# Neighbourhood attention in query blocks of 8 rows by 16 columns: key blocks of 12 by 32, values reloaded by block, one bias table per block

## The chip, the core and the metric

The kernel runs on one core of one Trainium2 chip. The metric is the time of one launch on the device, in microseconds (us). A core has engines that run their own instruction streams in order and wait for each other by semaphores: TensorE (PE, matrix products; its weight loads are listed as PEld), VectorE (DVE), ScalarE (ACT), GpSimd (POOL) and SyncE (SP, which here issues the DMA transfers). Engines compute on SBUF, 128 partitions wide; PE writes to PSUM banks of 512 fp32 columns.

## The reference

Two blocks run one after the other on 1024 tokens of width 1024. The first, in which the change lies, normalises the input, projects it, and joins two branches by an output projection: neighbourhood attention (8 heads of 64) and a gated delta rule (4 heads of 128, two directions). The tokens form a grid of 16 rows by 64 columns. Each query attends to a window of 8 rows by 16 columns around it, clipped at the borders, with a learned bias per offset:

```python
cs = np.clip(cols - NA_KW // 2, 0, GRID_W - NA_KW)      # 16 columns
rs = jnp.clip(r - kh // 2, 0, rows - kh)                # 8 rows
s = jnp.einsum('bhwd,bhiwjd->bhwij', q_r, k_sel).astype(jnp.float32) * scale + bias.astype(jnp.float32)
p = jax.nn.softmax(s.reshape(B, H, GRID_W, kh * NA_KW), axis=-1).reshape(s.shape).astype(v.dtype)
return jnp.einsum('bhwij,bhiwjd->bhwd', p, v_sel)
...
attn = _neighbourhood_attention(aq, ak, heads(av, NA_HEADS), rpb) * jax.nn.silu(az)
```

q and k are RMS-normalised per head with a gain. The delta rule needs, per chunk of 128, direction and head, inverses of triangular 64x64 blocks, their merging to 128x128, and a scan over the chunks. The second block (stick-breaking attention, retention, merge) is not touched.

## The kernel before

The program is written as loops of generators that are advanced in turn; a scheduler then fixes the order of each engine's instructions from its own model of their times, so the order around the change is not written out by hand.

The attention is made in four head pairs p. `na_proj(p)` (L479 to L524) projects q, k, v in token tiles of 128 (`dense_tok`, L102: fp32 values as a rounded part and a rest, three passes, 24 matmuls a tile) and the gate z in columns (L112, 48 matmuls of 512 columns). It squares (L496), sums (L498), takes the root on POOL, copies q, k, v out of PSUM on ACT (L501 to L503), scales q and k on DVE (L506), transposes k for four tiles at once (L514) and keeps it as rounded part and rest kS (L517, L518). It loads a bias table of 128x22x64 per head (L489).

`na_attn(p)` (L526 to L616) goes through eight query tiles of two grid rows, 128 queries. Its keys are eight whole grid rows, 512 columns; masked ones carry a large negative bias. Per tile q is doubled (L534), transposed (L537) and split (L539, L540). Per head two matmuls of 512 columns make the scores (L552); DVE adds the bias and takes the maximum (L560), negates it (L562), ACT takes the exponential and its sum (L563). Of four of the eight tiles the two rows have different windows: a second score matmul (L556) and short value matmuls (L589, evacuated at L598, added at L599) serve the eighth row. One tile later the probabilities are transposed (L569, four per head) and copied (L571), and multiplied with v (L583; each shows as two records, one per 64 columns of weights, in part). The sums' reciprocal (L591) is spread (L593), transposed (L594) and multiplied into the gate z (L595), which then multiplies the values (L600 or L602).

Other work runs between. `solver()` (L452 to L475) inverts by updates of X, each a product (L463) and an addition (L465), on DVE with buffer svt and on POOL with svq; the last rows on DVE with svq. The driver (L627 to L638) advances it four steps per tile of pairs 0 and 1, with the projection of the next pair; behind pair 1 comes `dz_raw` (L618), 192 matmuls of 256 columns. During pair 2 `merges()` (L655 to L693) makes eight merges, each a chain L668 (PE), L670 (ACT), L673 (PE), L676 (DVE), L679 (PE), L681 (ACT), for the last four also L687 (PE), in three PSUM banks "a" that the projections use too. During pair 3 the scan (L695 to L807) runs in 16 steps that each load 1.5 MB.

## Time and profile before

| | us |
|---|---|
| median of 3 runs (2333.69 to 2344.59) | 2336.43 |
| span of the profiled execution; no time of its own is recorded beside it | 2331.9 |
| PE busy | 2182.4 (94%) |
| DVE busy | 1414.8 (61%) |
| ACT busy | 863.7 (37%) |
| POOL busy | 1252.0 (54%) |
| DMA | 240.86 MB, mean 103 GB/s |

Busy times are sums over the whole span, and stages differ. The changed stage is about the fifth of the span between 300 and 760 us. A group's mean length is that of its instructions one by one; matmuls overlap, so the distance between two starts is shorter than a length.

### The profile page before, as it was taken

Reading aid. Unit: us, or ns where it says so; the run is one execution under the profiler, and the core shown is the slowest. Engines: PE = TensorE matmul, PEld = TensorE weight load, DVE = VectorE, ACT = ScalarE, POOL = GpSimd, SP = SyncE. Lnnn points to the kernel's source line nnn. Section 1 sums busy time; section 2 is a strip of 40 time slices with the busy share of each in tenths; the row PEclk is TensorE's granted clock in tenths of the full one; section 3 lists DMA queues with packets and bytes.
Section 4 is the critical chain, followed back from the end, with each engine's and each line's share of the span. In section 5 each row is a group of like instructions: output and inputs, shape, how many; then the busy total and the mean of one; then the engine's idle time right before and its main releaser. Section 6 shows DMA issues by size and latency. Waiting matters only on the chain.

```text
span 2331.9 us, 33715 instructions
## 1 busy us (share of the span) xinstructions
PE 2182.4 (94%) x12069; PEld 1864.4 (80%) x12069; DVE 1414.8 (61%) x2596; ACT 863.7 (37%) x2126; POOL 1252.0 (54%) x1467
## 2 busy tenths in 40 slices
PE   7998888999999999899889999999999999989999
PEld 7776877787888798787788777788888888767887
DVE  4688789844456568887877784426474744343221
...
GB/s 131 80 170 166 203 80 26 37 165 132 154 279 205 153 84 46 50 55 55 10 50 50 55 50 72 72 56 46 64 46 64 46 82 91 226 213 211 140 109 108
DMA packets 236488, 240.86 MB, mean 103 GB/s; under 512 B 39776, under 2 KB 173600, under 8 KB 236064
## 3 DMA queue, kind: packets, MB, share of 16 engines
...
q14 instruction: 73, 0.60, 0.1%
HBM read 167.31 MB, written 71.34 MB: 102 GB/s over the span
## 4 chain that ended last, share of the span: by engine, by line
PE 33%; DVE 16%; POOL 7%; issue 4%; DMA 4%; ACT 4%; SPq 0%; POOLq 0%; ACTq 0%; DVEq 0%
PE acc L112 21%; PE acc L102 5%; DVE qf L132 4%; PE acc L859 3%; DVE A L1039 3%; POOL A L1044 2%; DMA raw<-in_w_in_dram 1%; POOL wu L71 1%; DVE A L1035 1%; POOL ss L126 1%; DMA oa<-d_oa 1%; DVE ob L132 1%; DVE sq L988 1%; DVE wT L1058 1%; PE pt L1160 1%
## 5 line engine op out<-in xcount | busy, mean ns | idle before, releaser
L112 PE MATMUL acc<-h2h,wu 128*128 128x512 f32 x1504 | 459.1, 396 | 6.7 <-DVE sq L988 2.7
L102 PE MATMUL acc<-wu,h2h 128*128 128x384 f32 (+1 forms) x1536 | 376.2, 327 | 13.4 <-DVE sq L988 4.2
L71 POOL TENSOR_TENSOR wu<-raw,wu 128x512 fp32r<-128x512 f32 (+3 forms) x268 | 363.4, 1365 | 6.3
L70 POOL TENSOR_SCALAR wu<-raw 128x512 fp32r<-128x512 f32 (+3 forms) x268 | 205.9, 772 | 250.7 <-PE acc L112 176.7
L112 PEld LDWEIGHTS acc<-h2h,wu 128*128 128x128 f32 x1504 | 281.5, 188 | 71.9 <-ACT lg L956 3.1
L102 PEld LDWEIGHTS acc<-wu,h2h 128*128 128x128 f32 x1536 | 272.2, 194 | 21.5 <-issue 3.5
L112 PE MATMUL acc<-h2l,wu 128*128 128x512 f32 x752 | 276.1, 396 | 0.0
L102 PE MATMUL acc<-wu,h2l 128*128 128x384 f32 (+1 forms) x768 | 250.1, 327 | 0.0
L102 PE MATMUL acc<-wu,h1hi 128*128 128x384 f32 (+2 forms) x768 | 193.1, 335 | 12.6 <-DVE kS L518 6.7
L112 PE MATMUL acc<-h1hi,wu 128*128 128x512 f32 x512 | 164.3, 409 | 8.0 <-ACT pad L315 4.7
L112 PEld LDWEIGHTS acc<-h2l,wu 128*128 128x128 f32 x752 | 141.4, 188 | 31.0
L102 PEld LDWEIGHTS acc<-wu,h1hi 128*128 128x128 f32 x768 | 138.5, 196 | 17.0 <-issue 8.0
L1044 POOL TENSOR_TENSOR A<-Z,A 128x128 f32<-128x128 f32 (+2 forms) x96 | 112.4, 1176 | 70.5 <-DVE A L1039 43.6
L102 PEld LDWEIGHTS acc<-wu,h2l 128*128 128x128 f32 x768 | 148.4, 193 | 1.0
L102 PE MATMUL acc<-wu,h1lo 128*128 128x384 f32 (+2 forms) x384 | 127.8, 335 | 0.0
L112 PEld LDWEIGHTS acc<-h1hi,wu 128*128 128x128 f32 x512 | 98.1, 193 | 33.0 <-ACT pad L315 6.2
L126 POOL TENSOR_TENSOR ss<-ss,mhalf 128x2 f32<-128x2 f32 (+2 forms) x136 | 115.6, 851 | 7.2
L132 DVE STREAM_TRANSPOSE qf<-sq 32x256 f32<-32x256 f32 x256 | 111.6, 436 | 4.0
L125 POOL TENSOR_SCALAR ss<-ss 128x2 f32<-128x2 f32 (+2 forms) x136 | 42.5, 312 | 117.7 <-ACT sq L982 47.0
L1060 PE MATMUL po<-wT,v 128*128 128x512 f32 (+3 forms) x288 | 76.1, 365 | 22.2 <-DVE wT L1058 12.2
L112 PE MATMUL acc<-h1lo,wu 128*128 128x512 f32 x256 | 96.4, 405 | 0.0
L112 PE MATMUL acc<-oah,wu 128*128 128x512 f32 x256 | 81.3, 413 | 10.0 <-DVE sg L1232 6.1
...
## 6 DMA issues: line engine op xcount, KB each, us to landing
raw<-in_w_in_dram SPq DMA_DIRECT2D x192, 256.0 KB, 2.8
...
```

The source lines that it names most:

```text
L70: nc.gpsimd.tensor_scalar(out=u[:, 0, :], in0=raw, scalar1=1.0, scalar2=0.0, op0=ALU.mult, op1=ALU.add)
L71: nc.gpsimd.tensor_tensor(out=u[:, 1, :], in0=raw, in1=f32(u[:, 0, :]), op=ALU.subtract)
L102: nc.tensor.matmul(acc[:, :n], lhsT=hT[a][:, k, m * P:(m + 1) * P], rhs=us[k][:, b, c0:c0 + n], start=(k == 0 and i == 0), stop=(k == NK - ...
L112: nc.tensor.matmul(accs[half], lhsT=us[k][:, b, c0:c0 + P], rhs=hT[a][:, k, half * 512:(half + 1) * 512], start=(k == 0 and i == 0), stop= ...
L125: nc.gpsimd.tensor_scalar(out=dst, in0=src, scalar1=mul, scalar2=eps, op0=ALU.mult, op1=ALU.add)
L126: nc.gpsimd.tensor_tensor(out=dst, in0=dst, in1=mhalf[:, :eshape], op=ALU.pow)
L132: nc.vector.transpose(out=dst[32 * b:32 * b + 32, :, :, 32 * a:32 * a + 32], in_=src[32 * a:32 * a + 32, :, :, 32 * b:32 * b + 32])
L859: nc.tensor.matmul(acc, lhsT=us[k][:, y, (b % 4) * P:(b % 4 + 1) * P], rhs=token_set(mT[x][:, k, 0:T], s), start=(k == 0 and i == 0), stop ...
L988: nc.vector.scalar_tensor_tensor(out=sq[:, a * P:(a + 1) * P], in0=acc[:, a * P:(a + 1) * P], scalar=ss[:, a:a + 1], in1=gqk[:, a, :], op0 ...
L1039: nc.vector.tensor_tensor_scan(out=A[:, :w][:, ::-1], data0=A[:, :w][:, ::-1], data1=A[:, :w][:, ::-1], initial=0.0 if diag else ini[:, i4 ...
L1044: nc.gpsimd.tensor_tensor(out=A[:, :w], in0=Z[:, :w], in1=A[:, :w], op=ALU.subtract)
L1060: nc.tensor.matmul(po[:, i0 * P:512], lhsT=v[a][:, c0 // P + kb, :], rhs=wT[b][:, :n], start=(diag and kb == 0 and x == 0), stop=(diag == ...
```

## The change

A query tile becomes a block of 8 rows by 16 columns. All its windows lie in one key block of 12 rows by 32 columns, 384 columns, so there is one window per tile and no second matmuls. The bias comes as a table per tile for both heads, 128x2x384, with the mask in it, loaded tile by tile. Since a tile's keys are no run of tokens, v goes to DRAM (d_vn, 64 KB per token tile) and comes back by tile in the order of the key block (vb, four transfers of 32 partitions). q is normalised with its gain, doubled and transposed in the projection, four tiles at once, and kept as rounded part qH per head and rest qL. The probabilities are divided by their sum before they are transposed (one reciprocal and one scaling per head), so z is multiplied once. Line numbers move: L560 to L569, L563 to L572, L569 to L580, L583 to L591, L591 to L576, L668 to L664. The scratch memory for DMA descriptors and two tags of tiles that other stages reuse change names or size.

```diff
-    gq = load_const("qk_gain_q", [P, 1])
+    gqr = load_const("qk_gain_q", [P, 64], src=I["qk_gain_q"].partition_broadcast(P))
-    nc.vector.tensor_scalar_mul(out=gq, in0=gq, scalar1=0.125)
+    nc.vector.tensor_scalar_mul(out=gqr, in0=gqr, scalar1=0.125)
...
+    KR = (0, 4)
+    KC = (0, 8, 24, 32)
+    d_vn = dram.tile([4, T, P], F32, name="d_vn")
+    def blocks(ap):
+        return ap.rearrange("p (c r w) -> p r c w", c=4, r=8)
+    def rows(ap):
+        return ap.rearrange("p (r c w) -> p r c w", r=8, c=4)
     def na_proj(p, hold):
         us = load_units(I["w_in"], 128 * p, 128, parts=4, stride=512)
         pl = (na1, na)[p % 2]
-        qn = pl.tile([P, NM, P], F32, tag="qn", name="qn")
+        qH = [pl.tile([P, T], F32R, tag="qh%d" % hh, name="qH") for hh in range(2)]
+        qL = pl.tile([P, T], F32R, tag="ql", name="qL")
         kS = [pl.tile([P, T], F32R, tag="kS%d" % hh, name="kS") for hh in range(2)]
-        v = pl.tile([P, NM, P], F32, tag="v", name="v")
         z = pl.tile([P, T], F32, tag="z", name="z")
-        TB = []
-        for hh in range(2):
-            tb = na.tile([P, 22, 64], F32, tag="tb", name="tb", bufs=2)
-            nc.sync.dma_start(out=tb, in_=I["rpb"][2 * p + hh])
-            TB.append(tb)
-        hold.append((qn, kS, v, z, TB))
-        kns = []
+        hold.append((qH, kS, qL, z))
+        kns, qds = [], []
         for m, acc in dense_tok(hT, us, 0, 384):
             j = m % 4
             sq = na1.tile([P, 256], F32, tag="sq", name="sq", bufs=2)
             nc.scalar.activation(out=sq, in_=acc[:, 0:256], func=AF.Square)
+            raw = na1.tile([P, 384], F32, tag="raw", name="raw", bufs=2)
+            nc.scalar.copy(out=raw, in_=acc[:, 0:384])
+            nc.sync.dma_start(out=d_vn[p, m * P:(m + 1) * P, :], in_=raw[:, 256:384])
             ss = na1.tile([P, 4], F32, tag="ss", name="ss", bufs=2)
             nc.vector.tensor_reduce(out=ss, in_=sq.rearrange("p (h d) -> p h d", h=4), op=ALU.add, axis=AX.X)
             rsqrt_small(ss, ss, 1.0 / 64, EPS, 4)
             kn = na1.tile([P, P], F32, tag="kn", name="kn", bufs=5)
-            nc.scalar.copy(out=qn[:, m, :], in_=acc[:, 0:128])
-            nc.scalar.copy(out=kn, in_=acc[:, 128:256])
-            nc.scalar.copy(out=v[:, m, :], in_=acc[:, 256:384])
-            for x, t_ in enumerate((qn[:, m, :], kn)):
-                t_ = t_.rearrange("p (h d) -> p h d", h=2)
-                nc.vector.tensor_tensor(out=t_, in0=t_, in1=ss[:, 2 * x:2 * x + 2].unsqueeze(2).to_broadcast([P, 2, 64]),
-                                        op=ALU.mult)
+            nc.vector.tensor_tensor(out=kn.rearrange("p (h d) -> p h d", h=2), in0=raw[:, 128:256].rearrange("p (h d) -> p h d", h=2),
+                                    in1=ss[:, 2:4].unsqueeze(2).to_broadcast([P, 2, 64]), op=ALU.mult)
+            qd = na1.tile([P, 2, 2, 64], F32, tag="qd", name="qd", bufs=5)
+            for hh in range(2):
+                nc.vector.scalar_tensor_tensor(out=qd[:, hh], in0=raw[:, hh * 64:hh * 64 + 64].unsqueeze(1).to_broadcast([P, 2, 64]),
+                                               scalar=ss[:, hh:hh + 1], in1=gqr.unsqueeze(1).to_broadcast([P, 2, 64]),
+                                               op0=ALU.mult, op1=ALU.mult)
             kns.append(kn)
+            qds.append(qd)
             if j == 3:
                 sl = slice((m - 3) * P, (m + 1) * P)
-                # head 0 keeps its rounded part above the rest, head 1 the other way round
                 pt = bank("a")
                 for jj, k_ in enumerate(kns):
                     nc.tensor.transpose(pt[:, jj * P:(jj + 1) * P], k_, ident)
@@ -517,102 +528,87 @@
                     nc.scalar.activation(out=kS[hh][a, sl], in_=pt[a, :], func=AF.Copy, scale=gk[a])
                     nc.vector.scalar_tensor_tensor(out=kS[hh][b, sl], in0=pt[a, :], scalar=gk[a],
                                                    in1=f32(kS[hh][a, sl]), op0=ALU.mult, op1=ALU.subtract)
-                kns = []
+                for hh in range(2):
+                    a = slice(hh * 64, hh * 64 + 64)
+                    pt = bank("a")
+                    for jj, q_ in enumerate(qds):
+                        nc.tensor.transpose(pt[:, jj * P:(jj + 1) * P], q_[:, hh].rearrange("p x d -> p (x d)"), ident)
+                    nc.scalar.copy(out=blocks(qH[hh][:, sl]), in_=rows(pt))
+                    nc.vector.tensor_tensor(out=blocks(qL[a, sl]), in0=rows(pt[a, :]), in1=blocks(f32(qH[hh][a, sl])),
+                                            op=ALU.subtract)
+                kns, qds = [], []
             yield 1
         for half, acc in enumerate(dense_col(hT, us, 384)):
             last_na[0] = nc.scalar.activation(out=z[:, half * 512:half * 512 + 512], in_=acc, func=AF.Silu)
         yield 1
     def na_attn(p, tiles):
...
+        qH, kS, qL, z = tiles[p]
+        grid = lambda ap: ap.rearrange("p (r c) -> p r c", c=64)
+        def loads(t):
+            r, c = t // 4, t % 4
+            tb = na.tile([P, 2, 384], F32, tag="tb", name="tb", bufs=3)
+            nc.sync.dma_start(out=tb, in_=I["rpb"][p, t])
+            vb = na.tile([P, 3, P], F32, tag="vb", name="vb", bufs=3)
+            src = d_vn[p].rearrange("(g r c) d -> r c g d", r=4, c=64)
+            for i in range(4):
+                nc.sync.dma_start(out=vb[i * 32:i * 32 + 32], in_=src[i, KC[c]:KC[c] + 32, r:r + 3, :])
+            return tb, vb
+        def scores(t, hh, ld, rs2):
+            r, c = t // 4, t % 4
+            a = slice(hh * 64, hh * 64 + 64)
+            qs = lambda ap: ap[:, t * P:(t + 1) * P]
+            ks = lambda ap: grid(ap)[:, KR[r]:KR[r] + 12, KC[c]:KC[c] + 32]
             ps = bank("z")
...
+            nc.tensor.matmul(ps[:, 0:384], lhsT=qs(qH[hh]), rhs=ks(kS[hh]), start=True, stop=False)
+            nc.tensor.matmul(ps[:, 0:384], lhsT=qs(qL[a]), rhs=ks(kS[hh][a]), start=False, stop=True)
+            s = na.tile([P, 384], F32, tag="s", name="s", bufs=4)
             mx = na.tile([P, 1], F32, tag="mx", name="mx", bufs=4)
...
+            nc.vector.tensor_tensor_reduce(out=s, in0=ps[:, 0:384], in1=ld[0][:, hh, :],
                                            scale=1.0, scalar=-3.0e38, op0=ALU.add, op1=ALU.max, accum_out=mx)
             nc.vector.tensor_scalar_mul(out=mx, in0=mx, scalar1=-1.0)
             nc.scalar.activation(out=s, in_=s, func=AF.Exp, bias=mx, accum_out=rs2[:, hh:hh + 1])
...
+            return s
+        def transposed(s, rs2, hh):
+            nc.vector.reciprocal(out=rs2[:, hh:hh + 1], in_=rs2[:, hh:hh + 1])
+            nc.vector.tensor_scalar_mul(out=s, in0=s, scalar1=rs2[:, hh:hh + 1])
             pt = bank("t")
...
+            for i in range(3):
                 nc.tensor.transpose(pt[:, i * P:(i + 1) * P], s[:, i * P:(i + 1) * P], ident)
...
+            PT = na.tile([P, 384], F32, tag="PT", name="PT", bufs=3)
+            nc.scalar.copy(out=PT, in_=pt[:, 0:384])
             return PT
...
+        def values(t, ld, PTs):
+            r, c = t // 4, t % 4
+            po = bank("op"[t % 2])
+            for g in range(3):
                 for hh in range(2):
                     hs = slice(hh * 64, hh * 64 + 64)
...
+                    nc.tensor.matmul(po[hs, 0:P], lhsT=ld[1][:, g, hs], rhs=PTs[hh][:, g * P:(g + 1) * P],
+                                     start=(g == 0), stop=(g == 2))
+            zt = grid(z)[:, 8 * r:8 * r + 8, 16 * c:16 * c + 16]
+            nc.vector.tensor_tensor(out=zt, in0=po[:, 0:P].rearrange("p (r c) -> p r c", c=16), in1=zt, op=ALU.mult)
+        lds = [loads(0), loads(1)]
         prev = None
         for t in range(NM):
...
+            rs2 = na.tile([P, 2], F32, tag="rs2", name="rs2", bufs=3)
+            s0 = scores(t, 0, lds[t], rs2)
             if prev:
...
+                PTs = [transposed(prev[2], prev[4], 0)]
+            s1 = scores(t, 1, lds[t], rs2)
             if prev:
...
+                PTs.append(transposed(prev[3], prev[4], 1))
+                values(prev[0], prev[1], PTs)
+            if t + 2 < NM:
+                lds.append(loads(t + 2))
+            prev = (t, lds[t], s0, s1, rs2)
             yield 1
...
+        values(prev[0], prev[1], [transposed(prev[2], prev[4], 0), transposed(prev[3], prev[4], 1)])
         nc.sync.dma_start(out=d_att[p], in_=z)
```

The scheduler orders the program anew. On DVE, in pair 0, before, between solver updates (L463, L465): one tile's reciprocal, its spreading (rb), and the split of the next tile's q.

```order
L465 TENSOR_TENSOR X<-X,svt 128x10x35
L591 RECIPROCAL rs_3496<-rs_3496 128x2
L506 TENSOR_TENSOR qn<-qn,ss 128x128
L506 TENSOR_TENSOR kn<-kn,ss 128x128
L463 TENSOR_TENSOR svt<-X 128x360
L593 COPY rb<-rs_3496 128x128
L540 SCALAR_TENSOR_TENSOR qS<-pp,c_qk_gain_q,qS 128x256
L465 TENSOR_TENSOR X<-X,svt 128x10x36
L463 TENSOR_TENSOR svt<-X 128x324
L465 TENSOR_TENSOR X<-X,svt 128x9x36
```

After, a head's scores (s, mx), their negated maximum, reciprocal and scaling:

```order
L569 ISA s,mx<-pz,tb 128x384
L569 ISA mx 128x1
L463 TENSOR_TENSOR svt<-X 128x484
L571 TENSOR_SCALAR mx<-mx 128x1
L465 TENSOR_TENSOR X<-X,svt 128x44x11
L576 RECIPROCAL rs_2861<-rs_2861 128x1
L463 TENSOR_TENSOR svt<-X 128x264
L577 TENSOR_SCALAR s<-s,rs_2861 128x384
L465 TENSOR_TENSOR X<-X,svt 128x22x12
```

The reciprocal and the scaling of s now stand one or two solver updates behind the negation.

On PE, before, in pair 1: score (pz), value (pp) and transposing matmuls of a tile stand between matmuls of dz (wu, 256 columns).

```order
L552 MATMUL pz<-kS,qS 128x512 x2
L102 MATMUL acc<-wu,h1lo_99 128x256
L102 MATMUL acc<-wu,h1hi_98 128x256 x2
L552 MATMUL pz<-kS,qS 128x512 x2
L583 MATMUL pp<-PT,v 64x128 x2
L556 MATMUL pz<-kS,q_4319 64x64 x2
L583 MATMUL pp<-PT,v 64x128 x5
L589 MATMUL po<-PT,v 64x64 x4
L594 MATMUL pp<-ident,rb 128x128
L102 MATMUL acc<-wu,h1lo_99 128x256
L102 MATMUL acc<-wu,h1hi_98 128x256 x2
```

After, the end of pair 1: its gate columns (L112), the last transposes and the first value matmul, and the beginning of dz (256 columns):

```order
L112 MATMUL acc<-h1lo_99,wu 128x512 x2
L112 MATMUL acc<-h1hi_98,wu 128x512 x4
L112 MATMUL acc<-h1lo_99,wu 128x512 x2
L112 MATMUL acc<-h1hi_98,wu 128x512 x2
L580 MATMUL pt<-ident,s 128x128 x3
L591 MATMUL pp<-PT,vb 64x128
L102 MATMUL acc<-wu,h1hi_96 128x256 x2
```

The last five value matmuls of pair 1 stand 27 matmuls further on; behind them come 165 matmuls of dz without attention between, 32 of the projection of pair 3 with the scores of two tiles of pair 2 between them, and the first merge.

On PE, before, the first merge (its tiles tt, x1t, wt) and the work of the attention between its links:

```order
L668 MATMUL acc<-ident,tt 64x64 x8
L537 MATMUL po<-ident,qd 128x128 x2
L569 MATMUL pt<-ident,s 128x128 x4
L583 MATMUL pp<-PT,v 64x128
L673 MATMUL acc<-x1t,n_5227 64x64 x8
L552 MATMUL pz<-kS,qS 128x512 x4
L583 MATMUL pp<-PT,v 64x128 x7
L594 MATMUL pp<-ident,rb 128x128
L679 MATMUL acc<-tt,wt 64x64 x8
L668 MATMUL acc<-ident,tt 64x64 x8
```

After, the sixth merge, with nothing between its links:

```order
L664 MATMUL acc<-ident,tt 64x64 x8
L669 MATMUL acc<-x1t,n_5836 64x64 x8
L675 MATMUL acc<-tt,wt 64x64 x8
L683 MATMUL acc<-ident,tt 128x128 x8
L102 MATMUL acc<-wu,h1hi_96 128x384 x2
```

In the first four merges of the new order attention or projection stands between the links in part, in the last four hardly any.

## Rows read from the trace of the kernel before

**Rows 1.** Head of the page: span.
```profile
span 2331.9 us, 33715 instructions
```

**Rows 2.** Stretches: us; busy PE, PEld, DVE, ACT, POOL (xinstructions); PEclk, DMA share, GB/s.
```profile
300.00:460.00 160.00, 140.99 (x840) 119.22 (x839) 151.44 (x339) 65.14 (x179) 130.05 (x184) 0.95 0.14 44
460.00:520.00 60.00, 60.00 (x473) 52.60 (x471) 23.93 (x84) 25.92 (x62) 37.44 (x56) 1.00 0.47 140
520.00:620.00 100.00, 94.61 (x833) 78.70 (x833) 47.07 (x144) 55.48 (x135) 17.69 (x24) 0.98 0.42 127
620.00:760.00 140.00, 138.84 (x1067) 122.70 (x1066) 80.04 (x218) 68.79 (x183) 30.62 (x56) 1.00 0.70 243
```

**Rows 3.** Groups by line, 297 to 465: busy us, mean ns | idle before, releasers.
```profile
L465 DVE TENSOR_TENSOR X<-X,svt 128x294 f32<-128x294 f32 (+32 forms) x83 | 54.8, 661 | 1.4
L463 DVE TENSOR_TENSOR svt<-X 128x294 f32<-128x294 f32 (+32 forms) x83 | 53.0, 638 | 1.6
```

**Rows 4.** Timeline of PE, 655 to 675: start us, run us, line, tile, count.
```profile
656.15 0.60 PE L569 MATMUL pt<-ident,s 128*128 128x128 f32 x4
656.59 1.06 PE L719 MATMUL acc<-S,wsa 128*128 128x128 f32 x8
...
665.58 1.12 PE L583 MATMUL po<-PT,v 128*64 128x128 f32 x12
666.39 0.33 PE L589 MATMUL pp<-PT,v 64*64 64x64 f32 x4
...
666.76 0.33 PE L594 MATMUL po<-ident,rb 128*128 128x128 f32 x1
666.92 0.83 PE L740 MATMUL acc<-wsc,wsb 128*128 128x128 f32 x6
...
673.53 1.18 PE L552 MATMUL pz<-kS,qS 128*128 128x512 f32 x4
674.54 0.27 PE L569 MATMUL pt<-ident,s 128*128 128x128 f32 x1
```

**Rows 5.** Timeline of PE around the first merges, 519 to 529.
```profile
519.36 0.51 PE L102 MATMUL acc<-wu,h1hi 128*128 128x384 f32 x2
519.71 0.34 PE L102 MATMUL acc<-wu,h1lo 128*128 128x384 f32 x1
519.98 0.64 PE L668 MATMUL acc<-ident,tt 64*64 64x64 f32 x8
...
527.01 0.63 PE L668 MATMUL acc<-ident,tt 64*64 64x64 f32 x8 [0.67 <-ACT tt L681]
...
528.90 0.27 PE L673 MATMUL acc<-x1t,n 64*64 64x64 f32 x1 [0.46 <-ACT x1t L670]
```

**Rows 6.** Groups by line and shape, 290 to 740.
```profile
L563 ACT ACTIVATE s<-s,mx 128x512 f32<-128x512 f32 x64 | 46.0, 720 | 40.6 <-DVE mx L562 40.5
L552 PE MATMUL pz<-kS,qS 128*128 128x512 f32 x128 | 45.2, 444 | 0.8 <-ACT qS L539 0.6 <-DVE qS L540 0.2
L560 DVE CUSTOM_DVE_ANT_0 s<-pz,tb 128x512 f32<-128x512 f32 x64 | 42.2, 686 | 28.4 <-PE pz L552 15.3 <-PE pz L556 13.0
...
L593 DVE COPY rb<-rs 128x128 f32<-128x128 f32 x32 | 11.1, 348 | 0.4
...
L506 DVE TENSOR_TENSOR qn<-qn,ss 128x128 f32<-128x128 f32 x25 | 10.7, 426 | 5.6 <-POOL ss L126 5.3
L518 DVE SCALAR_TENSOR_TENSOR kS<-acc,c_qk_gain_k,kS 64x512 fp32r<-64x512 f32 x14 | 10.5, 750 | 1.6 <-ACT kS L517 1.3
...
L540 DVE SCALAR_TENSOR_TENSOR qS<-po,c_qk_gain_q,qS 128x256 fp32r<-128x256 f32 x16 | 7.7, 480 | 8.4 <-ACT qS L539 8.3
...
L591 DVE RECIPROCAL rs<-rs 128x2 f32<-128x2 f32 x32 | 5.1, 160 | 16.6 <-ACT s L563 16.4
```

**Rows 7.** The same over the whole span, a scaling in layer 2.
```profile
L1030 DVE TENSOR_SCALAR A<-Z 128x384 f32<-128x384 f32 x16 | 6.7, 420 | 6.3 <-PE pp L1055 3.5 <-ACT Z L1028 2.6
```

**Rows 8.** Line L593: durations ns min/median/max, first and last start.
```profile
L593 DVE COPY rb<-rs x32: 209/227/1665, 321.1 to 714.3; 128x128 f32<-128x128 f32 x32
```

More of the change, by code (lines that the diff above doesn't have):

```diff
@@ L574, in values @@
-        def values(t, st, PTs, pe):
-            po, qS, q2, rs2, rl, ru = st
-            v0 = rl // 2
-            steps = [(slice(0, P), slice(i * P, (i + 1) * P), v0 + i) for i in range(4)]
-            if rl != ru:
-                steps = steps[1:] + [(slice(64, P), slice(0, P), v0)]
-            for x, (ks, cs, vb) in enumerate(steps):
+            PT = na.tile([P, 384], F32, tag="PT", name="PT", bufs=3)
+            nc.scalar.copy(out=PT, in_=pt[:, 0:384])
+            return PT
+        def values(t, ld, PTs):
+            r, c = t // 4, t % 4
+            po = bank("op"[t % 2])
+            for g in range(3):
@@ L581, in values @@
                 for hh in range(2):
                     hs = slice(hh * 64, hh * 64 + 64)
-                    nc.tensor.matmul(po[hs, 0:P], lhsT=v[ks, vb, hs], rhs=PTs[hh][ks, cs], start=(x == 0), stop=(x == 3))
-            zt = z[:, t * P:(t + 1) * P]
-            if rl != ru:
-                for r in range(2):
-                    for hh in range(2):
-                        hs = slice(hh * 64, hh * 64 + 64)
-                        nc.tensor.matmul(pe[hs, P + r * 64:P + r * 64 + 64], lhsT=v[0:64, v0 + 4 * r, hs],
-                                         rhs=PTs[hh][0:64, r * 64:r * 64 + 64], start=True, stop=True)
@@ L610, in na_attn @@
             if prev:
-                PTs.append(transposed(prev[3]))
-                values(prev[0], prev[1], PTs, st[0])
-            prev = (t, st, s0, s1)
+                PTs.append(transposed(prev[3], prev[4], 1))
[3 more added lines that the diff above has]
+            prev = (t, lds[t], s0, s1, rs2)
             yield 1
-        values(prev[0], prev[1], [transposed(prev[2]), transposed(prev[3])], None)
+        values(prev[0], prev[1], [transposed(prev[2], prev[4], 0), transposed(prev[3], prev[4], 1)])
@@ L638, in tile_kernel @@
         dz_raw((range(0), range(0, NM))[p])
-    for g, tag in ((0, "z"), (1, "v")):
+    for g, tag in ((0, "z"), (1, "kS0")):
         zt = na.tile([P, 4, 2, P], F32, tag=tag, name="zt")
@@ L697, in scan @@
         tags = scan_tags
-        oparts = [na1.tile([P, 2, 4, P], F32, name="oacc", tag=tag) for tag in ("kS0", "kS1", "qn", "z")]
+        oparts = [na1.tile([P, 2, 4, P], F32, name="oacc", tag=tag) for tag in ("kS0", "kS1", "qh0", "z")]
         oacc = lambda n: oparts[n // 2][:, n % 2]
```

77 lines of the change are left out of this document (14 added, 63 removed).

## The prediction

> **What bounds the kernel now.** I read the page first: TensorE (PE) is busy almost throughout, so a change that removes matmuls looks like a gain. The reader should not stop there, because the share is a mean over stages. The changed stage lies between about 300 and 760 us of a span of 2331.9 us [rows 1]. I cut it where its other work changes [rows 2]. In stretch A, up to 520 us, attention of head pairs 0 and 1 runs beside the solver for the 64x64 inverses. In its first 160 us VectorE (DVE) is busy 151.44 us, 95%, against 140.99 of PE; from 460 to 520 PE is busy without a gap and DVE for 23.93 of 60 us. In B, 520 to 620, pair 2 runs beside the merges, and PE is busy 94.61 of 100. In C, 620 to 760, pair 3 runs beside the scan with PE busy 138.84 of 140, and there the DMA share is 0.70. So a matmul saved counts in C, counts in B if something else fills the merges' waits, and counts in A only where DVE is not the limit. Why DVE is full in A is in the groups of the solver: 54.8 + 53.0 us in two lines [rows 3].
>
> The sum is made against the span of the profiled execution; the median of the runs, 2336.43, lies 4.5 us above that, and I add these 4.5 at the end.
>
> **PE, removed and added.** I price by the distance between starts where matmuls stand packed, since their own lengths overlap. Four score matmuls of 512 columns take 674.54 - 673.53 = 1.01 us [rows 4], four transposes 0.44, and twelve value matmuls 0.81, 0.068 each; from the first value matmul of a tile with two row windows to its L594 it is 1.18, and L594 takes 0.16. A tile before is therefore 1.01 for scores, 0.07 for the second window's scores (four short ones on half of the tiles, priced at half a value matmul), 8 x 0.11 = 0.88 for transposes, 1.13 for values (16 x 0.068 = 1.08 or 1.18) and 0.16: 3.25 us. After, the scores have 384 columns; two L102 of 384 columns take 519.71 - 519.36 = 0.35 [rows 5], so four are 0.70; six transposes 0.66; twelve value matmuls 0.81. That is 2.17 us, 1.08 saved, 35 us over 32 tiles. The upper end is by the mean busy time: 444 ns for a score matmul [rows 6] would make it 1.78 instead of 1.01, but half of that is overlap; the ratio of 0.353 busy per matmul (45.2 / 128) to 0.253 is 1.4, which gives 1.5 per tile, 48 us. Groups of different matmuls rarely stand packed, so I take 1.3: 42 us in all, 10.4 per head pair. The q transposes move from the attention to the projection with equal count and cost nothing more.
>
> **DVE, removed and added, per tile** [rows 6]. Removed: a quarter of two L560, 2 x 0.686 x 0.25 = 0.34; qn (L506) 0.43; qS (L540) 0.48; rb (L593) 0.35; one multiply of z and, on half of the tiles, the addition L599, each priced as rb: 0.35 + 0.17. Sum 2.12. Added: two products for the normalised, doubled q (new L515), each at the price of qn, 0.86; qL, two instructions of 64x512 in four tiles at L518's 0.75, 0.38; one more reciprocal 0.16 (L591); and two multiplications of the probabilities, 128x384, which L1030 does in 0.42 [rows 7]: 0.84. Sum 2.24. DVE is given 0.12 us more per tile: what PE is spared, DVE is not. For L577 I hold 0.2 to 1.7 as bounds, the shortest and longest rb [rows 8]; 0.42 is the nearest row, of its exact shape.
>
> [...]
>
> **Stretch A.** DVE is busy 151.44 + 23.93 = 175.4 us there. The order shows that the solver's tail on svq, 20 small instructions, now stands behind pair 1's last tile; at half the mean of the solver's lines [rows 3], 0.33 each, these are 6.5 us. Up to pair 1's last scaling DVE has 169 us, plus 16 x 0.12 = 2. Its idle time of 160 - 151.44 = 8.6 I halve, since L560 waits for PE above all (28.4 us in the whole stage [rows 6]) and PE is lighter. So the last scaling comes at 300 + 171 + 4 = 475. Behind it PE still has, by the order: 48 matmuls of z with 512 columns (0.23 each from the 0.175 of 384 columns, 11.2 us), 192 of dz with 256 columns (0.117 each, 22.4), which before stood between the tiles, 32 of 384 columns (5.6), and scores and transposes of two tiles (3). These 42 us run alone, less 2 beside the last tile: the first merge comes at 515, against 519.98 [rows 5]. Of 16 tiles x 1.3 = 21 us, 5 arrive. The granted clock is 0.95 in the first part of A, where PE has gaps, and 1.00 where it has none [rows 2]; more gaps may lower it, which is hidden as long as DVE leads.
>
> **Stretch B.** Saved 10.4. Each merge is a chain of PE, ACT, PE, DVE, PE, ACT; before, attention and projection stand between the links. The distance from the end of L668 (527.01 + 0.63) to L673 at 528.90 is 1.26 us [rows 5], a link with its evacuation. The new order has merges 4 to 7 with most links back to back: about 11 unfilled links, 13.9 us. Of these 5.4 are not new, PE being idle 100 - 94.61 before [rows 2]. The twelve k and q transposes in one batch go through the three banks that the merges use also: two more links, 2.5. Sum 10.4 + 5.4 - 13.9 - 2.5, about -0.6.
>
> **Stretch C.** Saved 10.4. The eight tables (393 KB) and eight value blocks (197 KB) less two old tables (721 KB) are 3.3 MB more, where 0.70 of the DMA moves 243 GB/s [rows 2]: at full share 9.4 us. Nothing lost and 9.4 lost are the bounds; since 0.30 is free I take 3. The loads stand in order on SP two tiles ahead with three buffers; if one waits for its buffer, the scan's loads queue behind it. +7.4.
>
> ACT loses copies and a quarter of the exponentials and evacuations; at 65.14 of 160 us in A it is no bound, and I count nothing. GpSimd (POOL) has nothing new.
>
> **Sum.** 5 - 0.6 + 7.4 = 12: span 2320, and 2324 with the 4.5 us outside.
>
> **Rivals.**
> 1. The PE saving arrives whole. For it: PE's share in B, C and from 460. It needs DVE in A to get room, by L577 and L515 costing half. 42 us less: 2294. Against it: dz behind the tiles.
> 2. Slower: DVE waits for the exponential. Before, one reciprocal a tile (L591) stands well behind its exponentials, and still waited 16.4 us for ACT. Now reciprocal and scaling of each head can stand one or two solver instructions, 0.65 us each [rows 3], behind L571, while the exponential alone takes 0.720 us [rows 6] and its accumulator is read after it. The solver's next instructions are queued behind such a wait on DVE, POOL's half of the solver behind those, and PE's transposes behind the scaling. With 32 in A, the 12 us of gain are gone from 0.4 us each on; at 0.8 us each, 26 us, the time is 2350.
> 3. DVE and POOL get in each other's way: rb takes 0.209 to 1.665 us, mean 0.348, without other cause in its shape [rows 6, 8], beside POOL's solver. If each of the 32 scalings in A pays 0.5 us for it, 16 us: 2340; bounds 0.14 (4.5 us) and 1.46 (47 us). [...]
> 4. Nothing to measure: the links of B and the DMA of C eat the 12 us. DMA at its upper bound (-6), five links more in B (-6): 2336.
>
> **How the numbers follow.** Forecast 0.48 (its own range 2313 to 2335), rival 1 0.20, rival 2 0.16, rival 3 0.06, rival 4 0.10. Half a per cent, 11.7 us, is about what can be told from no change: faster is below 2324.7, slower above 2348. The forecast lies at that border: 0.28 of it is faster, 0.20 no change. Rival 1 gives 0.19 to faster and 0.01 to no change, rival 2 0.16 to slower, rival 3 0.03 each to no change and slower, rival 4 0.08 to no change and 0.02 to slower. Faster 0.47, no change 0.32, slower 0.21. For 8 in 10 the range reaches over rival 1 without its tail and to rival 2's 2350: 2295 to 2350.
>
> **What would show it.** In the profile after: PE's busy time in A falls by some 20 us while the first merge (new L664) comes only 5 us earlier; dz (L102, 128x256) stands in one block without attention between; L576's idle time is put on ACT and is small (over 12 us in A speaks for rival 2); L577 has a mean near 0.42 us (over 0.9 speaks for rival 3); the waits of PE for the merges' evacuations grow by 8 to 11 us; the last tile of pair 3 ends some steps earlier in the scan. The prediction is wrong if the first merge moves by more than 10 us either way.

## The result

The changed kernel is slower: 2362.27 us (median of 4 runs, 2355.85 to 2366.43) against 2335.06 before; the ratio is 1.0111, 95% interval 1.0093 to 1.0130. The forecast was 2324, with a range up to 2350. The profiled execution has a span of 2354.1 us, 22.2 more than before [rows 1].

The stretches cut at the same times as [rows 2], of the kernel after (columns as there):

```profile
300.00:460.00 160.00, 147.95 (x728) 114.93 (x729) 155.47 (x361) 54.77 (x130) 109.42 (x157) 0.89 0.31 92
460.00:520.00 60.00, 56.91 (x356) 47.67 (x355) 33.45 (x90) 15.69 (x36) 40.91 (x68) 0.94 0.32 94
520.00:620.00 100.00, 90.46 (x656) 75.63 (x656) 38.76 (x121) 37.39 (x82) 27.51 (x34) 0.91 0.65 188
620.00:760.00 140.00, 135.33 (x991) 117.55 (x990) 78.28 (x215) 59.34 (x158) 21.43 (x42) 0.95 0.72 239
```

DVE is still full up to 460 and now also busy for 33.45 us behind it, instead of 23.93. PE is hardly less busy than before, although it has fewer and narrower matmuls, and its granted clock is lower in every stretch: 0.89, 0.94, 0.91, 0.95 against 0.95, 1.00, 0.98, 1.00.

To split the 22 us, three marks (matmul lines of the merges' first link, of the scan's first product and of the output projection, each with lengths in ns, first and last start), of the kernel after:

```profile
L664 PE MATMUL acc<-ident,tt x64: 216/216/247, 535.3 to 635.4; 64*64 64x64 f32 x64
...
L715 PE MATMUL acc<-S,wsa x96: 275/275/377, 665.8 to 738.9; 128*128 128x128 f32 x96
...
L855 PE MATMUL acc<-mahi,wu x128: 392/397/498, 743.6 to 847.9; 128*128 128x512 f32 x128
```

and of the kernel before:

```profile
L668 PE MATMUL acc<-ident,tt x64: 216/216/300, 520.0 to 612.0; 64*64 64x64 f32 x64
...
L719 PE MATMUL acc<-S,wsa x96: 275/275/377, 636.9 to 715.5; 128*128 128x128 f32 x96
...
L859 PE MATMUL acc<-mahi,wu x128: 387/394/505, 721.0 to 826.3; 128*128 128x512 f32 x128
```

| stretch | before | after | difference | forecast |
|---|---|---|---|---|
| A, 300 to the first merge | 220.0 | 235.3 | +15.3 | -5 |
| B, to the scan's first product | 116.9 | 130.5 | +13.6 | +0.6 |
| C, to the output projection | 84.1 | 77.8 | -6.3 | -7.4 |

C came close to its forecast. A and B failed.

**The scores.** PE around one head's scores, and line by line the weight loads before them (PEld rows: idle before in us, and what ended it):

```profile
409.96 0.34 PE L102 MATMUL acc<-wu,h1hi 128*128 128x384 f32 x1
410.13 0.34 PE L565 MATMUL pz<-kS,qH 128*128 128x384 f32 x1
410.40 0.44 PE L566 MATMUL pz<-kS,qL 64*128 64x384 f32 x1
410.77 0.44 PE L102 MATMUL acc<-wu,h1hi 128*128 128x384 f32 x1
411.06 0.34 PE L102 MATMUL acc<-wu,h1lo 128*128 128x384 f32 x1
```

```profile
L566 PEld LDWEIGHTS pz<-kS,qL 64*128 64x128 f32 x64 | 12.7, 199 | 14.1 <-issue 14.0
```

Two L102 of the same 384 columns stand 0.17 us apart, as in [rows 5]. The second score matmul starts 0.27 behind the first, the next L102 0.37 behind that, and even the L102 after it is late by 0.12: 0.93 for three matmuls instead of 0.52. The weight load of L566 waits 14 us in all, 0.22 each, for nothing that the trace names. Over the 62 pairs from 300 to 744 in which L566 comes right behind L565, the two distances add up to 0.75 us in the median.

**DVE.** The groups of pairs 0 and 1 (300 to 489), then of pairs 2 and 3 (520 to 744), with busy us and mean ns, and then the scaling in the whole span (shortest, median and longest in ns):

```profile
L515 DVE SCALAR_TENSOR_TENSOR qd<-raw,ss,c_qk_gain_q 128x128 f32<-128x128 f32 x36 | 18.6, 552 | 0.0
...
L569 DVE CUSTOM_DVE_ANT_0 s<-pz,tb 128x384 f32<-128x384 f32 x33 | 17.9, 545 | 0.4 <-PE pt L580 0.2
L577 DVE TENSOR_SCALAR s<-s,rs 128x384 f32<-128x384 f32 x33 | 17.8, 545 | 0.1
```

```profile
L577 DVE TENSOR_SCALAR s<-s,rs 128x384 f32<-128x384 f32 x31 | 15.5, 501 | 0.7
...
L515 DVE SCALAR_TENSOR_TENSOR qd<-raw,ss,c_qk_gain_q 128x128 f32<-128x128 f32 x16 | 4.9, 345 | 0.0
```

```profile
L577 DVE TENSOR_SCALAR s<-s,rs x64: 403/420/1428, 310.7 to 712.6; 128x384 f32<-128x384 f32 x64
```

Against [rows 6] and [rows 7], from which 0.43 and 0.42 us were taken: the products for q take 552 ns beside the solver and 345 without it, the scaling 545 and 501. These means mix two cases. The 38 scalings during which POOL runs nothing take 0.403 to 0.423 us, as forecast; the 26 that overlap a POOL instruction take 0.407 to 1.428, 0.68 in the mean. From 300 to 744, q's products take 0.337 to 0.347 us alone and up to 0.770 beside POOL. Instructions of DVE that read PSUM show no such difference: qL (L537) takes 0.69 in both cases, and the maximum of the scores (L569) 0.53 to 0.56.

The end of pair 1 on DVE:

```profile
488.95 0.45 DVE L577 TENSOR_SCALAR s<-s,rs 128x384 f32<-128x384 f32 x1
505.78 0.29 DVE L594 TENSOR_TENSOR z<-pp,z 128x128 f32<-128x128 f32 x1 [16.39 <-PE pp L591]
509.39 0.39 DVE L463 TENSOR_TENSOR svq<-X 128x224 f32<-128x224 f32 x1 [3.31 <-POOL X L465]
```

The last scaling ends at 489.4 (starts at 488.95), where 475 was forecast. Then DVE waits 16.39 us for the last value matmuls, which PE reaches only behind the gate columns and 27 matmuls of dz, and the solver's tail is queued behind that wait.

**The merges.** PE around the sixth merge (in brackets the idle time before, and what ended it):

```profile
595.39 0.63 PE L664 MATMUL acc<-ident,tt 64*64 64x64 f32 x8
596.77 1.14 PE L669 MATMUL acc<-x1t,n 64*64 64x64 f32 x16 [0.75 <-ACT x1t L666]
598.70 1.14 PE L675 MATMUL acc<-tt,wt 64*64 64x64 f32 x16 [0.79 <-DVE wt L672]
600.64 1.94 PE L683 MATMUL acc<-ident,tt 128*128 128x128 f32 x8 [0.80 <-ACT tt L677]
602.24 0.99 PE L102 MATMUL acc<-wu,h1hi 128*128 128x384 f32 x2
603.02 0.52 PE L102 MATMUL acc<-wu,h1lo 128*128 128x384 f32 x1
```

The second link of [rows 5] waited 0.46; here each waits 0.75 to 0.80 us with PE idle, and behind the merge two L102 take (603.02 - 602.24) / 2 = 0.39 instead of 0.17. In two stretches:

```profile
570.00:600.00 30.00, 25.06 (x208) 21.89 (x207) 8.46 (x19) 8.18 (x18) 3.44 (x6) 0.88 0.41 116
600.00:648.00 48.00, 42.35 (x254) 37.18 (x255) 19.20 (x52) 12.36 (x28) 4.74 (x8) 0.75 0.29 83
```

the granted clock is 0.88 and 0.75; in pieces of 4 us it is 0.50 from 588 to 592, from 600 to 604 and from 640 to 644, and 1.00 from 608 to 612 and from 620 to 628. Over all of B it is 0.88, before 0.99. PE's waits at the links (us in total, times, longest):

```profile
PE acc L675 <- DVE wt L672: 3.2, 4, 0.9
PE acc L669 <- ACT x1t L666: 3.0, 4, 0.9
...
PE acc L683 <- ACT tt L677: 2.4, 3, 0.8
```

That is eleven waits of 8.6 us, 0.78 each; before there were two, 1.1 us.

### The profile page after: what moved, and what is told of

Its sections match the earlier page's. It is cut to its first block, busy times and chain, and to the rows that moved or that the text cites. A ratio compares the mean times of both kernels' runs of the same rounds, so it can differ in the third digit from the quotient of the medians.

```text
span 2354.1 us, 33101 instructions
## 1 busy us (share of the span) xinstructions
PE 2189.6 (93%) x11653; PEld 1851.2 (79%) x11653; DVE 1441.3 (61%) x2628; ACT 822.7 (35%) x1980; POOL 1244.9 (53%) x1467
## 4 chain that ended last, share of the span: by engine, by line
PE 47%; DVE 25%; POOL 9%; issue 6%; DMA 6%; ACT 5%; SPq 1%; POOLq 0%; DVEq 0%; ACTq 0%
PE acc L112 25%; PE acc L102 8%; DVE qf L132 4%; PE acc L855 3%; DVE A L1035 3%; POOL ss L126 2%; DVE X L465 2%; POOL A L1040 2%; DVE cv L320 2%; DVE svt L463 1%; DVE A L1031 1%; POOL wu L71 1%; DMA raw<-in_w_in_dram 1%; POOL wu L70 1%; DMA oa<-d_oa 1%
## 5 line engine op out<-in xcount | busy, mean ns | idle before, releaser
L112 PE MATMUL acc<-h2h,wu 128*128 128x512 f32 x1504 | 459.8, 396 | 8.0 <-DVE sq L984 3.4
L102 PE MATMUL acc<-wu,h2h 128*128 128x384 f32 (+1 forms) x1536 | 373.3, 326 | 15.7 <-DVE sq L984 4.7
L112 PEld LDWEIGHTS acc<-h2h,wu 128*128 128x128 f32 x1504 | 281.4, 188 | 74.3 <-ACT lg L952 4.4
L102 PEld LDWEIGHTS acc<-wu,h2h 128*128 128x128 f32 x1536 | 269.7, 192 | 23.8 <-issue 3.5
L112 PE MATMUL acc<-h2l,wu 128*128 128x512 f32 x752 | 276.2, 396 | 0.0
L102 PE MATMUL acc<-wu,h2l 128*128 128x384 f32 (+1 forms) x768 | 248.7, 325 | 0.0
L102 PE MATMUL acc<-wu,h1hi 128*128 128x384 f32 (+2 forms) x768 | 196.3, 338 | 10.1 <-ACT pad L315 2.7
L112 PE MATMUL acc<-h1hi,wu 128*128 128x512 f32 x512 | 167.4, 417 | 6.6 <-ACT pad L315 3.7
L112 PEld LDWEIGHTS acc<-h2l,wu 128*128 128x128 f32 x752 | 141.4, 188 | 31.2
L102 PEld LDWEIGHTS acc<-wu,h1hi 128*128 128x128 f32 x768 | 137.4, 196 | 17.3 <-POOL wu L71 4.2
L102 PEld LDWEIGHTS acc<-wu,h2l 128*128 128x128 f32 x768 | 147.4, 192 | 1.1
L112 PEld LDWEIGHTS acc<-h1hi,wu 128*128 128x128 f32 x512 | 101.3, 199 | 33.9 <-ACT pad L315 5.3
L102 PE MATMUL acc<-wu,h1lo 128*128 128x384 f32 (+2 forms) x384 | 126.2, 332 | 0.0
L112 PE MATMUL acc<-h1lo,wu 128*128 128x512 f32 x256 | 98.3, 414 | 0.0
L112 PE MATMUL acc<-oah,wu 128*128 128x512 f32 x256 | 81.7, 415 | 8.7 <-DVE sg L1228 5.2
```

The costliest lines, as they stand in the source:

```text
L102: nc.tensor.matmul(acc[:, :n], lhsT=hT[a][:, k, m * P:(m + 1) * P], rhs=us[k][:, b, c0:c0 + n], start=(k == 0 and i == 0), stop=(k == NK - ...
L112: nc.tensor.matmul(accs[half], lhsT=us[k][:, b, c0:c0 + P], rhs=hT[a][:, k, half * 512:(half + 1) * 512], start=(k == 0 and i == 0), stop= ...
```

## The experiments

The theories: A, the strided keys make the scores slow; E, the 64 rows of weights do; B, DVE's added work sets the end of pair 1; C, the block of dz does; F, the merges' unfilled links and the clock behind them cost the rest; D, the added transfers do.

The time of each is given as the ratio to the kernel before, run beside it. The changed kernel's own ratio is 1.0111 (1.0093 to 1.0130).

| run | ratio (95% interval) | first to last L664 or its like |
|---|---|---|
| changed kernel | 1.0111 (1.0093 to 1.0130) | 535.3 to 635.4 |
| e1_contig | 1.0077 (1.0051 to 1.0104) | 545.1 to 640.4 |
| e1b_runs96 | 1.0107 (1.0090 to 1.0124) | 534.2 to 635.1 |
| e2_noscale | 1.0071 (1.0045 to 1.0098) | 528.6 to 625.3 |
| e6_nodma | 1.0089 (1.0068 to 1.0109) | 535.0 to 636.9 |
| e8_k128 | 1.0065 (1.0049 to 1.0082) | 532.2 to 634.3 |
| e5_dzB | 1.0160 (1.0143 to 1.0177) | 541.0 to 643.7 |
| e7_comboB | 1.0075 (1.0053 to 1.0097) | 523.5 to 624.7 |
| e9_all | 1.0011 (0.9999 to 1.0023) | 518.5 to 622.4 |
| e7_combo0 | 1.0048 (1.0029 to 1.0067) | 525.6 to 623.9 |
| e10_nodzB | 0.9998 (0.9982 to 1.0014) | 521.7 to 620.0 |
| e10_links0 | 0.9955 (0.9940 to 0.9971) | 522.6 to 608.2 |
| e10_links | 0.9963 (0.9949 to 0.9978) | 516.5 to 612.6 |
| e11_links | 1.0085 (1.0061 to 1.0108) | 535.9 to 635.2 |
| e3_actscale | 1.0080 (1.0054 to 1.0106) | 525.6 to 624.8 |

### What makes the scores slow

e1_contig and e1b_runs96 change what the scores read:

```diff
-            ks = lambda ap: grid(ap)[:, KR[r]:KR[r] + 12, KC[c]:KC[c] + 32]
+            ks = lambda ap: ap[:, KR[r] * 64:KR[r] * 64 + 384]                     # e1_contig
+            ks = lambda ap: ap.rearrange("p (s x) -> p s x", s=4)[:, :, KR[r] * 16:KR[r] * 16 + 96]   # e1b_runs96
```

> The scores read 384 keys that lie side by side instead of 12 rows of 32 (so these are the wrong keys; nothing else changes). Theory A, the strided reading makes a score matmul slow: the distance from L565 to L566 and on falls from 0.27 and 0.37 us to about 0.18 each, 128 x 0.2 = 25 us less of PE time, of which the half outside the DVE-bound stretch shows: 2345 to 2352. Rival, the second matmul's 64-row weights or the switch to them make it slow: the distances stay, time 2358 to 2366.

> The scores read four runs of 96 neighbouring keys instead of twelve of 32 (wrong keys again). If the cost is one per run of neighbours, the distances lie near the contiguous ones, about 0.22 us, and the time a few us above that kernel's. If any pattern that is not contiguous costs twice, they stay at 0.27 and 0.37 and the time at 2358 to 2366.

Theory A fell. With neighbouring keys L565 to L566 is still 0.27 us:

```profile
411.78 0.34 PE L565 MATMUL pz<-kS,qH 128*128 128x384 f32 x1
412.05 0.44 PE L566 MATMUL pz<-kS,qL 64*128 64x384 f32 x1
```

Over all such pairs the two distances add up to 0.74 in the median, as in the changed kernel. The time of e1_contig lies lower, its median of 2352 at the end of theory A's range, but its interval overlaps that of the changed kernel, and its instructions are ordered otherwise in some places (the first merge comes 10 us later, the scan's end earlier); the distances are what decides. e1b_runs96 is like the changed kernel.

e8_k128 gives the second matmul 128 rows of weights:

```diff
-        qL = pl.tile([P, T], F32R, tag="ql", name="qL")
+        qL = [pl.tile([P, T], F32R, tag="ql%d" % hh, name="qL") for hh in range(2)]
...
-            nc.tensor.matmul(ps[:, 0:384], lhsT=qs(qL[a]), rhs=ks(kS[hh][a]), start=False, stop=True)
+            nc.tensor.matmul(ps[:, 0:384], lhsT=qs(qL[hh]), rhs=ks(kS[hh]), start=False, stop=True)
```

> qL is kept per head on all 128 partitions, so that both score matmuls have 128 rows; to make room the bias table has two buffers instead of three and the residual uses other tiles' space. Theory E, a matmul with 64 rows of weights between ones with 128 lets no weight load run ahead: the distances from L565 and L566 fall from 0.27 and 0.37 us to 0.18 to 0.2, 128 x 0.19 = 24 us less of PE time, half of it where PE sets the time: 2346 to 2352. Rival, the scores are slow for what their weights or keys are and not for the number of rows: the distances stay, 2358 to 2366.

PE around one head's scores, and the weight loads, in e8_k128:

```profile
408.97 0.34 PE L565 MATMUL pz<-kS,qH 128*128 128x384 f32 x1
409.14 0.34 PE L566 MATMUL pz<-kS,qL 128*128 128x384 f32 x1
409.32 0.33 PE L102 MATMUL acc<-wu,h1hi 128*128 128x384 f32 x1
```

```profile
L566 PEld LDWEIGHTS pz<-kS,qL 128*128 128x128 f32 x64 | 13.4, 209 | 0.2 <-issue 0.2
```

The distances are 0.17 and 0.18, as L102's, with the keys read in twelve runs of 32; the weight load's idle time is 0.2 us in all. So it was the 64 rows (theory E); why they cost this is not shown beyond the weight load's idle time. Not every pair gets down to 0.35: behind transposes and value matmuls L565 to L566 still takes 0.26 to 0.28, and the two distances add up to 0.46 in the median, instead of 0.75. The time falls by 0.46%, 11 us, as expected.

### DVE

e2_noscale leaves the two lines of reciprocal and scaling out.

> Reciprocal and scaling of the probabilities are left out (the output is not divided by the sums). Theory B, DVE's work sets the end of pair 1: 16 tiles x 2 x (0.54 + 0.15) = 22 us less of DVE there, the first merge (L664 before) comes 15 to 22 us earlier than 535, time 2338 to 2348. Rival C, PE's block of dz and the merges' links set it: the first merge moves by under 6 us, time 2355 to 2362.

Pair 0 ends 18 us earlier (its output is written at 408.2 instead of 426.5), more than the 11 us of DVE time taken out of its eight tiles, so DVE and the chain through it set the pace there. At the end of pair 1 the gate columns begin at 474.7 instead of 488.3. But the first merge moves by only 6.7 us, and the time falls by 0.40%, to 2350.6: both lie between the two theories' ranges, and the interval just overlaps the changed kernel's. Behind pair 1's last tile PE's own work takes over (30.00 of 30 us busy from 490 to 520), and the order moved too: ten heads of pair 2 are scored ahead of the first merge instead of five, so its place is no clean mark here. e3_actscale puts only the scaling on ACT, e7_combo0 also q's two products, with q's gain multiplied into k's:

```diff
-            nc.vector.tensor_scalar_mul(out=s, in0=s, scalar1=rs2[:, hh:hh + 1])
+            nc.scalar.activation(out=s, in_=s, func=AF.Copy, scale=rs2[:, hh:hh + 1])     # both
...
-                nc.vector.scalar_tensor_tensor(out=qd[:, hh], in0=raw[...], scalar=ss[:, hh:hh + 1], in1=gqr[...], ...)
+                nc.scalar.activation(out=qd[:, hh], in_=raw[...], func=AF.Copy, scale=ss[:, hh:hh + 1])   # e7_combo0
```

> Of the two kinds of DVE work moved away before, only the scaling of the probabilities (L577) goes to ACT; q's products (L515) stay on DVE. If both kinds weigh by their time, 0.54 us each and two a tile, half of the 14 us: 2353 to 2358. If the scaling's place in the chain from exponential to transposes matters more than its time: 2348 to 2351.

> DVE relieved alone: scaling of the probabilities and q's two products on ACT, q's gain multiplied into k's; dz stays behind pair 1 and the second score matmul keeps its 64 rows. Theory B, DVE's added work sets the end of pair 1: 2.2 us a tile less, the first merge at 510 to 522 instead of 535, time 2340 to 2350. Rival C, the block of dz and the order set it: the first merge at 530 or later, time 2355 or more.

e3_actscale gains 0.31% and e7_combo0 0.63%, 7 and 15 us, each in the range for which both kinds weigh by their time. Only e7_combo0 is clear of the changed kernel's interval; e3_actscale's overlaps both. And the first merge lies at 525.6 in both, just above the 510 to 522 expected of e7_combo0. So DVE's added work costs time, but that q's products weigh as the scaling does is not shown.

### The block of dz

e5_dzB takes the projection three steps a tile in pair 1's first four tiles, and dz two steps a tile in the last four:

```diff
-            take(prj, 1)
-        drain(prj)
-        dz_raw((range(0), range(0, NM))[p])
+            if p == 0:
+                take(prj, 1)
+            elif t < 4:
+                take(prj, 3)
+            else:
+                take(dzg, 2)
+        drain(prj)
+        drain(dzg)
```

> In pair 1 the projection of pair 2 is taken three steps a tile in the first four tiles, and dz two steps a tile in the last four, so that dz stands between the last tiles' work. Theory C, the block of dz behind pair 1 costs time: the first merge comes 10 to 20 us earlier than 535, time 2340 to 2350. Theory B, DVE sets the end of pair 1 and PE then has as much left: the first merge moves by under 5 us, time 2356 to 2366.

Theory C fell: dz stands between the transposes and values of the last tiles then, and the time rises by 0.5%, the first merge comes 5.7 us later. The time, 2374, lies above both ranges. With DVE relieved (e7_comboB) and with 128 rows as well (e9_all) it makes no clear difference either:

> As the kernel before with dz in pair 1, and DVE relieved: the scaling of the probabilities goes to ACT, and q's gain is multiplied into k's, so that q's two products go to ACT as well. DVE loses 2 x 0.54 + 2 x 0.54 = 2.2 us a tile, 35 us in pairs 0 and 1, and PE has its filler between the tiles. Theories B and C together: the first merge at 500 to 510, time 2325 to 2338. If the clock or the merges' links set the rest, 2345 to 2355.

> The kernel with dz in pair 1 and DVE relieved, and both score matmuls with 128 rows as well. If theories B, C and E each hold: 12 us below the one without the 128 rows, 2313 to 2328, and below the kernel before (2335). If E does not hold, as that one.

> DVE relieved and both score matmuls with 128 rows, dz behind pair 1 as in the changed kernel. If moving dz forward costs time, as its run alone says (12 us slower), this is faster than the version with dz between the tiles: 2322 to 2332. If dz between the tiles helps once DVE is relieved: 2340 to 2348.

e7_comboB and e7_combo0 differ in dz alone, as do e9_all and e10_nodzB; both pairs' intervals overlap. e7_comboB missed its first range: the first merge comes at 523.5, not by 510, and the time, 2352, lies in the range given for the clock or the links. e9_all was expected below the kernel before, e10_nodzB below it or above; both miss their ranges and reach it, 1.0011 and 0.9998: the two causes found so far, DVE's work and the 64 rows, are worth 1.1% together and bring the kernel back to where it came from, without a gain.

### The merges' links

The merges yield after each link, and half a tile of pair 2 or a token tile of projection is issued between:

```diff
             nc.scalar.copy(out=x1t, in_=pa[0:64, :])
+            yield 1
...
             nc.vector.tensor_copy(out=wt[64:128, :], in_=pb[64:128, :])
+            yield 1
...
-    for t, _ in enumerate(na_attn(2, cur)):
-        take(mg_, 1)
-        take(prj, 1)
+    for y in na_attn(2, cur):          # pair 2 yields 0 after its first head, 1 after the tile
+        if y == 0:
+            take(mg_, 1)
+            take(prj, 1)
+            take(mg_, 1)
+        else:
+            take(mg_, 1)
```

> The version before this one, and the merges issued link by link with half a tile of attention or a token tile of projection between the links, so that PE has filler in most of them. Theory F, unfilled links and the lower clock behind them cost the rest: the merges take 90 to 95 us from the first to the last instead of 100 to 104, PE's granted clock from 560 to 650 is 0.95 or more instead of 0.77 to 0.89, and the time is 8 to 12 us below the version before. Rival, the merges are bound by their loads and by POOL's memset: the same time within 4 us.

> The links filled, with dz between pair 1's tiles: by theory F 8 to 12 us below the same kernel without filled links (2337.7), 2325 to 2330; by the rival 2334 to 2341.

> The changed kernel with nothing but its merges issued link by link (DVE and the scores as changed). If the unfilled links and the clock behind them cost by themselves what they gave on the relieved kernel: 8 to 12 us below 2362, 2350 to 2354, and the granted clock from 570 to 650 at 0.9 or more instead of 0.75 to 0.88. If the links matter only once DVE is relieved: 2358 to 2364.

e10_links0 is 0.43% below e10_nodzB, 10 us, and 0.45% below the kernel before; its interval excludes 1. e10_links, with dz between pair 1's tiles, is 0.48% below e9_all, in theory F's range. From the first to the last merge e10_links0 takes 85.6 us instead of 98.3. The scan's first product does not come earlier (648.8, and 647.8 in e10_nodzB); what fills the links is work of pair 3, whose output is written at 675.7 instead of 716.0, and so the scan stage takes 714.2 - 648.8 = 65.4 us instead of 80.3. PE around one of the last four merges, and the stretches, of e10_links0:

```profile
591.79 1.14 PE L674 MATMUL acc<-x1t,n 64*64 64x64 f32 x16
592.86 0.55 PE L582 MATMUL pt<-ident,s 128*128 128x128 f32 x3
593.34 0.43 PE L593 MATMUL pp<-PT,vb 128*64 128x128 f32 x2
593.77 1.11 PE L681 MATMUL acc<-tt,wt 64*64 64x64 f32 x16
594.81 0.87 PE L593 MATMUL pp<-PT,vb 128*64 128x128 f32 x10
595.64 1.06 PE L689 MATMUL acc<-ident,tt 128*128 128x128 f32 x8
```

```profile
570.00:600.00 30.00, 28.78 (x242) 25.27 (x241) 9.27 (x24) 13.89 (x35) 5.16 (x9) 1.00 0.50 138
600.00:650.00 50.00, 42.05 (x296) 33.31 (x296) 23.53 (x80) 31.61 (x71) 0.00 (x0) 0.95 0.84 257
```

None of the links shown waits, and the clock is 1.00 and 0.95. In all merges three waits at links for another engine are left, 2.6 us, where e10_nodzB has seven, 5.5. On the changed kernel alone the same edit (e11_links) gives 0.26%, 6 us, under the 8 to 12 expected, and its interval overlaps the changed kernel's; the clock is 0.89 in both stretches, just under the 0.9 named, and the merges take 99.3 us as before; what it gains is again in the scan stage (735.8 - 674.2 = 61.6 us instead of 77.8), less a scan that begins 8 us later. There six waits at links are left, 4.8 us. Theory F holds on the relieved kernel; on the changed one its gain is not clear of the noise. Links and clock were changed together, so which share is whose is not shown.

### The transfers

e6_nodma loads tables and values of a pair's first tile only.

```diff
-        lds = [loads(0), loads(1)]
+        lds = [loads(0)] * NM
...
-            if t + 2 < NM:
-                lds.append(loads(t + 2))
```

> The bias table and the values of tile 0 serve all eight tiles of a pair, so 28 table loads and 112 value loads are left out (wrong values). Theory D, the added transfers cost time, in the scan above all: 2350 to 2355. Rival, they lie beside other work: 2358 to 2366, and the stage from the first scan step to the output projection keeps its 78 us.

The time is that of the changed kernel within the intervals, and from the scan's first product (667.2) to the output projection (745.0) it takes 77.8 us, as in the changed kernel. The transfers cost nothing that can be told.

## Why the prediction was wrong

1. "After, the scores have 384 columns; two L102 of 384 columns take 0.35, so four are 0.70" is the step that failed on PE. The price was that of a matmul with 128 rows of weights; the new L566 has 64. A head's two matmuls cost 0.93 - 0.17 = 0.76 us instead of 0.35, so a tile 1.52 instead of 0.70. Of the 1.08 saved per tile, 0.26 is left. e8_k128 shows the row count as the cause of most of it; with 128 rows a tile's scores take 0.92 by the median, so 0.70 would not have been met either. The prediction named the half-size operand nowhere: it priced by columns alone.
2. "DVE is given 0.12 us more per tile" is the step that failed in A. Measured against the taken prices: q's products 0.55 instead of 0.43 each, the scaling 0.545 instead of 0.42 each, k's scaling 0.45 instead of the former 0.30 (its shape is unchanged; the forecast left it out) and the score maximum saves 0.28 instead of 0.34. That is 0.24 + 0.25 + 0.15 + 0.06 = 0.70 more, 11 us in 16 tiles. DVE's busy time up to 520 rose from 175.4 to 188.9, 13.5 us where 2 were forecast, and the last scaling is 14 us late. The mechanism, DVE as the limit of A, was right; its size was off. What was missing is the time beside POOL: 0.42 is what the scaling takes alone (the lower bound of 0.2 was reached by none, the shortest took 0.403), and rows 6 mixed pairs beside the solver with pairs without it. PE stood close behind: with scaling and q's products off DVE (e7_combo0) the first merge comes only 10 us earlier.
3. "About 11 unfilled links, 13.9 us", set off against a saving of 10.4 in B: eleven links do wait, 0.78 us each instead of 1.26, so the forecast's net of 13.9 - 5.4 = 8.5 came out as 8.6 - 1.1 = 7.5 (filling them gave 10 us in e10_links0, 6 in e11_links). But the saving against them was only 8 x 0.26 = 2 us instead of 10.4, and in this stretch the granted clock fell to 0.75, for which the forecast had no term in B. As an estimate of that term: in pieces of 1 us the clock in B is 0.50 in 25, 1.00 in 95 and between the two in 10, so that with a mean of 0.88 it was 0.50 for 31 of B's 130.5 us; by 0.39 against 0.17 us for the same 384 columns, PE's work in them would take some 14 us at 1.00, up to 17 less (PE idled in part of it). The lost saving and the clock together are more than the 13 us by which B missed; how they share it was not separated.
4. Stretch C came out at -6.3 against -7.4, though from other parts: the transfers cost nothing (e6_nodma), and the scores saved less. What made up for it at least in part is work that had moved: behind the scan's first product stand the scores of six tiles before (24 L552) and of four after (8 L565).
5. The tail of PE behind pair 1's last scaling was forecast as 42 us less 2, and is 535.3 - 489.4 = 46.

**The rivals.** Rival 1 (the whole saving arrives) fell with point 1. Rival 2, the slower one of the list, gave the right direction for a wrong reason: DVE's waits for the exponential come to 0.6 us in pairs 0 and 1 and 10.3 in the whole stage (the same group from 300 to 489 and from 280 to 760),

```profile
L576 DVE RECIPROCAL rs<-rs 128x1 f32<-128x1 f32 x33 | 4.9, 152 | 0.7 <-ACT s L572 0.6
```

```profile
L576 DVE RECIPROCAL rs<-rs 128x1 f32<-128x1 f32 x64 | 9.8, 155 | 10.4 <-ACT s L572 10.3
```

far from the 12 in A named as its sign. Rival 3 named the scaling. Its mean of 0.545 is far from the 0.9 named as its sign, and 0.13 above what it takes alone, near the rival's lower bound of 0.14; but that DVE takes longer beside POOL is what the rows show, in the scaling, in q's products, 0.552 beside POOL's work and 0.345 in pairs 2 and 3, and in the solver itself. DVE and POOL at one place in pair 0:

```profile
331.90 0.49 DVE L463 TENSOR_TENSOR svt<-X 128x324 f32<-128x324 f32 x1
...
332.43 1.46 DVE L465 TENSOR_TENSOR X<-X,svt 128x324 f32<-128x324 f32 x1
...
334.62 1.48 DVE L465 TENSOR_TENSOR X<-X,svt 128x342 f32<-128x342 f32 x1
336.02 0.77 DVE L577 TENSOR_SCALAR s<-s,rs 128x384 f32<-128x384 f32 x1
```

```profile
331.96 1.58 POOL L71 TENSOR_TENSOR wu<-raw,wu 128x512 fp32r<-128x512 f32 x1
...
334.16 1.57 POOL L71 TENSOR_TENSOR wu<-raw,wu 128x512 fp32r<-128x512 f32 x1
335.70 0.88 POOL L70 TENSOR_SCALAR wu<-raw 128x512 fp32r<-128x512 f32 x1
```

An X update of 324 columns takes 1.46 us where the solver's product of the same size just before takes 0.49. Both slow updates and the scaling begin behind a POOL instruction and end shortly after it: 332.43 + 1.46 = 333.89 against 331.96 + 1.58 = 333.54, 334.62 + 1.48 = 336.10 against 334.16 + 1.57 = 335.73, and 336.02 + 0.77 = 336.79 against 335.70 + 0.88 = 336.58. What makes them take longer there is not shown beyond that. In e1_contig, e8_k128 and e11_links the scaling spreads in the same way (0.40 us at the shortest, 0.42 in the median, 1.48, 1.43 and 1.43 at the longest). No run here moves POOL's work, so the cause is read from the rows and not tried. Rival 4's DMA fell with e6_nodma.
